# Row factors of blocks 2 and 3: from diagonal matrices on TensorE to a store in DRAM and a broadcast load

## The chip, the cores and the metric

The kernel runs on one core of one Trainium2 chip. The metric is device time in microseconds (us) of one execution; lower is better. Before the change three runs took 2093.21, 2093.47 and 2093.49 us, so the median is 2093.47 us. The engines are called PE (TensorE, matrix products), DVE (VectorE), ACT (ScalarE), POOL (GpSimd) and SP (SyncE, which here only issues DMAs).

## The reference

One layer of a pre-norm residual trunk over x of 2048 rows and 1024 columns, all in float32:

```python
h = rmsnorm(x, norm_mix_g)                      # x * rsqrt(mean(x*x) + EPS) * g, per row
u = einsum('bsd,dc->bsc', h, w_in)              # 1024 -> 3584 columns
gate_b, gate_c, v, x_r, g = split(u)
y_conv = gate_b * causal_dwconv(gate_c * v, conv_w)
y_rnn  = rg_lru(causal_dwconv(x_r, rnn_conv_w) + rnn_conv_b, ...) * gelu(g)
x = x + concat[rmsnorm(y_conv), rmsnorm(y_rnn)] @ w_out
x = x + square(relu(rmsnorm(x) @ W1)) @ W2      # 1024 -> 4096 -> 1024
out = rmsnorm(x, final_norm_g)
```

What the change touches is the factor of the first `rmsnorm`: for each row s of x one number, rsqrt(mean of x[s]^2 + EPS).

## The kernel before, in words

The 2048 rows are cut into four blocks of 512 (`TB`), and the blocks are worked in two pairs, (0, 1) and then (2, 3). Each pair goes through the mixers, the product with `w_out`, and the MLP (`mlp(b, ...)` with b = 0 and b = 2). The MLP of the first pair is the time from about 466 to 1066 us; it has an "up" half (`Up`, product with W1, matmuls on line 653) and a "down" half (`Down`, product with W2, line 771). Each matrix product is made of seven smaller products over the two blocks of a pair instead of eight (the numbers `i` in `ORDER = (1, 2, 6, 5, 7, 3, 4)`), and each of these of three passes over a high and a low part of the float32 operands (`w_hi`, `w_lo`, `z_hi`, `z_lo`, `H`), which ACT casts and DVE subtracts (`split_into`, lines 197 and 198). The loop of the up half is `for n in range(...)` over 56 pairs (s, i); its last seven, n = 49 to 55, belong to s = 7, and one of them is 24 matmuls.

While the MLP of the first pair runs, work for the second pair is put in between. One part of it is the row factors of blocks 2 and 3. The table `FACTORS` says at which n of the up half what is done: `next_rows(k, part)` loads a quarter of the rows of block k (tile `xq`), `next_part(k, 0..3)` lets ACT square and sum it, and `next_part(k, 4)` makes the factors (`norm_rows`, seven tiny DVE instructions and a root on ACT, ending in tile `rs_x`, 128 partitions x 4: row t*128 + p of the block is at partition p, column t).

The second pair's normalization works on the transposed rows `xT`, with the 512 rows of a block along the free dimension and the same factor wanted on all 128 partitions. So the factors have to be turned from 128 x 4 into one row of 512 and repeated on every partition (`bcs`, one tile of 128 x 512 for each of the two blocks). Before the change `next_part(k, 6)` makes four diagonal matrices (`diagonal`, lines 410 and 411 on DVE, high and low part, tiles `diag_hi` and `diag_lo` out of the pool `temp`), and `next_part(k, 8)` multiplies a matrix of ones with them on PE (`spread`, line 428, two matmuls into a PSUM tile `bc`) and lets ACT copy the result into `bcs` (line 1018). The consumer, `next_scale` (line 1021, instructions on line 435), runs near the end of the first pair's MLP.

What sets the order: inside `mlp` PE's order is the order of the code (`manual_schedule` for PE alone); the order of DVE, ACT, POOL and SP is chosen by the framework's scheduler when the kernel is built. Every engine then takes its instructions strictly in that order. SP issues nearly all DMAs through one queue: the spills `d_z<-snap` and `d_z<-z` of the up half (line 581), the weight loads `w<-in_w_mlp_in_dram` (line 613), and a background stream of loads and stores that prepares the second pair's weights (`prepare_sums`, lines 1624 and 1636, tiles `w_in`, `sum_hi`, `d_sum`). An instruction of SP that waits holds up all DMAs behind it. Tiles of `temp` come out of a pool of 27, weight tiles (`wtile`) out of 15, PSUM tiles out of 4.

Of the kernel before, what the change touches and what calls it, by code (L numbers as in the profile page):

```python
# [9 lines left out]
F32 = mybir.dt.float32  # L10
# [5 lines left out]
P = 128  # L16
# [3 lines left out]
TB = 512  # L20
NB = SEQ // TB
NT = TB // P
# [36 lines left out]
FACTORS = {}  # L59
for k in range(2):  # L60
    for n in range(4):
        FACTORS.setdefault(12 + 8 * n + 4 * k, []).append((True, 2 + k, n))
        FACTORS.setdefault(17 + 8 * n + 4 * k, []).append((False, 2 + k, n))
    for n in range(3):
        FACTORS.setdefault(46 + k + 2 * n, []).append((False, 2 + k, 4 + 2 * n))
PAIR_UNITS = "c0 g1 v0 x0 x1 x2 g0 x3 g2 b0 g3 c1 v1 b1".split()
PAIR_ITEMS = "c0.0 g1.0 bc1 hv00 hv0.0 G1.0 g1.1 G0.0 c0.1 x0.1 x1.1 v0.1 G0.1 x2.1 G1.1 x2.0 "
PAIR_ITEMS += "g0.1 x3.1 G2.0 x3.0 g2.1 g2.0 G2.1 b0.1 G3.0 b0.0 g3.1 G3.1 c1.0 g3.0 v1.0 b1.0 "
# [23 lines left out]
def block_kernel(  # L92
# [14 lines left out]
    nc = tc.nc  # L107
# [16 lines left out]
    dp = ctx.enter_context(  # L124
        tc.tile_pool(name="dp", bufs=2, space=bass.MemoryType.DRAM)
    )
# [14 lines left out]
    def psum(name, shape=(P, 2, TB)):  # L141
        return psp.tile(list(shape), F32, tag="ps", name=name)
# [4 lines left out]
    def small(name):  # L147
        return sp.tile([P, NT], F32, tag=name, name=name)
# [274 lines left out]
    def spread(diag, n, ps=None):  # L423

        if ps is None:
            ps = psum("bc", (P, n * P))
        for i, d in enumerate(diag):
            nc.tensor.matmul(
                ps, ones_r, d.rearrange("p n q -> p (n q)"), start=i == 0, stop=i == 1
            )  # L430
        return ps
# [13 lines left out]
    with tc.manual_schedule(  # L445
# [10 lines left out]
        for q in range(4):  # L456
            n, ks = q // 2, slice(2 * (q % 2), 2 * (q % 2) + 2)
# [38 lines left out]
        diag = diagonal(norm_rows(s2, NT), NT)  # L496
# [491 lines left out]
    bcs = [cp.tile([P, TB], F32, name="bcs%d" % i) for i in range(2)]  # L988
    factors = {}
    nxt = {}  # L990
# [9 lines left out]
    def next_part(b, n, ps=None):  # L1000

        nxt = factors.setdefault(b, {})
        if n == 0:
            nxt["s2"] = [small("s2_%d%d" % (b == NB - 1, i)) for i in range(2)]
        if n < 4:
            th, dh = n // 2, n % 2
            r = nxt.pop(n)
            for k in range(2):
                c = 2 * th + k
                nc.scalar.activation(  # L1010
                    r[:, k], r[:, k], AF.Square, accum_out=nxt["s2"][dh][:, c : c + 1]
                )
        elif n == 4:
            nxt["rs"] = norm_rows(nxt["s2"], NT)
        elif n == 6:
            nxt["diag"] = diagonal(nxt["rs"], NT)
        elif n == 8:
            nc.scalar.copy(bcs[b == NB - 1], spread(nxt["diag"], NT, ps))

    def next_scale(b, q):  # L1020
        scale_rows(xtt[b, q], 2 * q, bcs[b == NB - 1], 2)
# [1415 lines left out]
    def mlp(b, ups, r0, r1, t2, rest, xs, turns_at, prepared):  # L2437
        Z = {}
        in_mlp.append(b)
        seq = [(s, i) for s in range(3) for i in ORDER[:2]]  # L2440
        seq += [(s, i) for s in range(3) for i in ORDER[2:]]
        seq += [(s, i) for s in range(3, NS) for i in ORDER]
        downs = [Down(s) for s in range(NS // 2)]
        for n in range(-LEAD1, len(seq)):
            m = n + LEAD1
            if prepared <= m < len(seq):
                ups[seq[m][0]].prepare(seq[m][1])
            m = n + SUMS1
            if 0 <= m < len(seq):
                ups[seq[m][0]].sums(seq[m][1])  # L2450
            if n == -LEAD1:
                if prepared < 3:
                    ups[1].load((0,))
                ups[0].load((1,))
            if n < 0:
                continue
            s, i = seq[n]
            ups[s].multiply(i, H)
            if s == NS - 1 and i in (3, 4):
                with tc.issue_after(made_at["snap"]):  # L2460
                    downs[0].prepare(1, i - 3)
            ups[s].drain(i, Z)
            if n == 0:
                ups[2].load((0,))
            for t in turns_at.get(n, ()):
                rest(t, xs[t])
            if n == 4:
                ups[1].load((1,))
            later_operands(n, r0, r1, t2)
            if i == 5 and s >= 2 and s + 1 < NS:  # L2470
                ups[s + 1].load()
            if b < PAIRED:
                for fn, k, at in FACTORS.get(n, ()):
                    (next_rows if fn else next_part)(k, at)
            if b < PAIRED and BG_FROM <= n < len(seq) - 6 and i != 3:
                step()
            if i == 3 and s == 0:
                ups[2].load((1,))
            if s == NS - 1:
                if i in (1, 2):  # L2480
                    if i == 2:
                        downs[0].fetch(1, 0, Z)
                        downs[0].fetch(1, 1, Z)
                    downs[0].load(i - 1, hp.tile([P, 4, 2, 512], F32, tag="h", name="w2_first"))
                if i == 6:
                    downs[0].fetch(2, 0, Z)
                    downs[0].fetch(2, 1, Z)
                if i == 5:
                    downs[0].sums(0)
                if i == 7:  # L2490
                    downs[0].sums(1)
                    downs[0].fetch(6, 0, Z)
                if i == 3:
                    for th in range(2):
                        xt[b, th, 0] = refill("x2", keep_x[b, th, 0])

        more = b + 2 < NB
        seq = [(s, i, a) for s in range(NS // 2) for i in ORDER for a in range(2)]
        fetched = 5
        for n in range(-LEAD2, len(seq)):  # L2500
            m = n + LEAD2
            if m < len(seq):
                s, i, a = seq[m]
                if m > 1:
                    downs[s].prepare(i, a)
                if s and a == 0 and i in (1, 2):
                    downs[s].sums(i - 1)
                if a == 0 and i in (6, 5):
                    downs[s].last_sum(i == 5)
            for at, bb, dh in ((1, b, 1), (3, b + 1, 1), (9, b + 1, 0)):  # L2510
                if n == at:
                    for th in range(2):
                        xt[bb, th, dh] = refill("x2", keep_x[bb, th, dh])
            if n < 0:
                continue
            while fetched < min(n + LEAD2 + 3, len(seq)):
                s, i, a = seq[fetched]
                downs[s].fetch(i, a, Z)
                fetched += 1
            s, i, a = seq[n]  # L2520
            end = s == NS // 2 - 1
            if not (end and i == 4):
                downs[s].multiply(i, a)
                if a == 1:
                    downs[s].drain(i, b)
            elif a == 1:
                downs[s].multiply_last((ends[1].tiles if more else ends[1].last_tiles)(ends[0]))
            if i == 7 and s + 1 < NS // 2:
                downs[s + 1].load(a)
            if more and n > 6 and (s < 2 or s == 2 and i != 4):  # L2530
                step()
            if more and s == NS // 2 - 1:
                if (i, a) == (6, 1):
                    load_xt(b + 2)
                    hw = first_operands()
                if i in (7, 3):
                    q = 2 * (i == 3) + a
                    next_scale(b + 2, q)
                    split_first(hw, q, xtt[b + 2, q])
                if (i, a) == (3, 0):  # L2540
                    load_xt(b + 3)
                if i == 4:
                    for q in (2 * a, 2 * a + 1):
                        next_scale(b + 3, q)
            if end and (i, a) == (5, 0):
                ends = [Finish(b, 0), Finish(b + 1, 1)]
                ends[0].first()
            if end and (i, a) == (3, 1):
                if more:
                    for t in range(NT):  # L2550
                        ends[0].add(t, None)
                else:
                    stated[0] = True
                    ends[0].halves()
            if end and (i, a) == (7, 1):
                ends[1].first()
        if more:
            xr0, xr1 = ([xtt[b + 2 + n, q] for q in range(4)] for n in range(2))
            xt2 = [temp("T2") for _ in range(2)]
            for q in range(2):  # L2560
                other_sums(xr0, xr1, xt2, q)
            split_pair(6, xt2)
            hs["r"] = xr0, xr1, xt2
# [61 lines left out]
```

## Time and profile before

| | |
|---|---|
| runs | 2093.21, 2093.47, 2093.49 us |
| profiled execution | 2093.85 us; 2092.0 us of it from the first to the last instruction (span) |
| PE busy | 2082.5 us of the span |
| DVE, ACT busy | 1621.5 us, 1143.4 us |
| DMA | 226 GB/s mean over the span |
| granted TensorE clock | 0.999 |

Lines of the profile read so: in a timeline, start and duration in us, engine, line of the kernel, operation, out<-in, and in brackets the idle time before it and what ended it; in a list of waits, total us, times, longest; SPq is the DMA queue of SP, and the duration there is that of issuing. `L653` is line 653 of the kernel.

### The profile page before, as it was taken

The numbers are of one execution on the slowest core, as the hardware profiler recorded it, in microseconds if no ns is written. First come the engines' busy times: TensorE is split into PE (matmuls) and PEld (weight loads), VectorE is DVE, ScalarE is ACT, GpSimd is POOL, SyncE is SP. The second block draws the span as 40 slices with busy tenths as digits, with TensorE's granted clock in tenths as the row PEclk, the third lists the DMA queues.
The fourth block names the chain that finished last, engine by engine and source line by source line (L and its number), as shares of the span: only waits on it lengthen the run. The fifth ranks groups of instructions, "written<-read, shape, count | busy, mean of one in ns | idle before, by whom it ended". The sixth has DMA issues, their size and how long they took to land.

```text
span 2092.0 us, 25032 instructions
## 1 busy us (share of the span) xinstructions
PE 2082.5 (100%) x9328; PEld 1714.5 (82%) x9328; DVE 1621.5 (78%) x1844; ACT 1143.4 (55%) x1509; POOL 47.3 (2%) x75
## 2 busy tenths in 40 slices
PE   9999999999999999999999999999999999999998
PEld 8888788888888888888888887888888888888887
DVE  5789898569776878999987776875875665887776
ACT  6789863377655544443555887235853333333344
POOL 0011000000000000000000100000000000000000
PEclk9999999999999999999999999999999999999999
DMA  9489688743788788777384557675343445844432
GB/s 341 163 295 331 240 329 344 267 164 116 262 313 285 263 296 306 266 288 280 121 312 164 209 181 270 243 271 181 131 181 119 166 158 211 328 165 151 141 121 81
DMA packets 198760, 473.56 MB, mean 226 GB/s; under 512 B 14960, under 2 KB 79472, under 8 KB 198640
## 3 DMA queue, kind: packets, MB, share of 16 engines
q1 hardware_dynamic: 197040, 467.25, 61.6%
q10 hardware_dynamic: 1568, 4.72, 0.6%
q8 instruction: 73, 1.20, 0.2%
q14 instruction: 47, 0.39, 0.1%
q0 software_dynamic: 32, 0.00, 0.0%
HBM read 313.58 MB, written 158.33 MB: 226 GB/s over the span
## 4 chain that ended last, share of the span: by engine, by line
PE 82%; DVE 7%; ACT 4%; issue 2%; DMA 1%; POOL 0%; SPq 0%; DVEq 0%; ACTq 0%; POOLq 0%
PE up L653 41%; PE dn L771 27%; PE wo_x L2082 6%; PE wo_w L2082 3%; PE wo_y L2082 2%; DVE xr L1289 1%; DVE v L1346 1%; PE ps_b L256 1%; ACT r L1310 1%; PE psri L1757 1%; DVE w_lo L1230 1%; ACT gi L1317 1%; PE ps_c L256 1%; PE ps_v L256 1%; PE dn L790 1%
## 5 line engine op out<-in xcount | busy, mean ns | idle before, releaser
L653 PE MATMUL up<-H,w_hi 128*128 128x512 f32 x2576 | 795.2, 390 | 0.1
L653 PEld LDWEIGHTS up<-H,w_hi 128*128 128x128 f32 x2576 | 482.3, 188 | 103.0 <-issue 1.8
L653 PE MATMUL up<-H,w_lo 128*128 128x512 f32 x1288 | 501.5, 389 | 0.0
L771 PE MATMUL dn<-w_lo,z_hi 128*128 128x512 f32 x864 | 336.2, 389 | 0.8 <-DVE w_lo L198 0.8
L771 PE MATMUL dn<-w_hi,z_lo 128*128 128x512 f32 x864 | 336.1, 389 | 0.0
L771 PE MATMUL dn<-w_hi,z_hi 128*128 128x512 f32 x864 | 336.1, 389 | 0.0
L653 PEld LDWEIGHTS up<-H,w_lo 128*128 128x128 f32 x1288 | 241.8, 188 | 51.3 <-DVE w_lo L198 1.0
L197 ACT CAST z_hi<-z 128x1024 fp32r<-128x1024 f32 x112 | 118.1, 1054 | 299.9 <-PE dn L771 243.1
L198 DVE TENSOR_TENSOR w_lo<-w,w_hi 128x1024 fp32r<-128x1024 f32 x156 | 190.0, 1220 | 73.5 <-ACT w_hi L197 25.2
L197 ACT CAST w_hi<-w 128x1024 fp32r<-128x1024 f32 x156 | 163.0, 1049 | 114.8 <-PE up L653 48.2
L771 PEld LDWEIGHTS dn<-w_lo,z_hi 128*128 128x128 f32 x864 | 162.2, 188 | 34.7 <-DVE w_lo L198 1.2
L771 PEld LDWEIGHTS dn<-w_hi,z_lo 128*128 128x128 f32 x864 | 162.2, 188 | 33.8
L771 PEld LDWEIGHTS dn<-w_hi,z_hi 128*128 128x128 f32 x864 | 162.2, 188 | 33.7
L803 DVE TENSOR_TENSOR x<-dn,x 128x1024 f32<-128x1024 f32 x108 | 130.9, 1218 | 19.1 <-PE dn L771 19.0
L198 DVE TENSOR_TENSOR z_lo<-z,z_hi 128x1024 fp32r<-128x1024 f32 x112 | 136.2, 1216 | 4.8 <-ACT z_hi L197 4.8
L2082 PE MATMUL wo_x<-w_o,y_hi 128*128 128x512 f32 x384 | 119.5, 392 | 0.0
L665 ACT COPY snap<-up 128x1024 f32<-128x1024 f32 x48 | 48.7, 1015 | 63.4 <-PE up L653 57.1
L2082 PEld LDWEIGHTS wo_x<-w_o,y_hi 128*128 128x128 f32 x384 | 71.0, 188 | 14.5 <-DVE x L2095 0.4
L2082 PE MATMUL wo_x<-w_o,y_lo 128*128 128x512 f32 x192 | 75.0, 390 | 0.0
L670 ACT ACTIVATE snap<-snap 128x1024 f32<-128x1024 f32 x33 | 35.0, 1060 | 60.0 <-DVE snap L694 22.1
L2082 PE MATMUL wo_w<-w_o,y_hi 128*128 128x512 f32 x192 | 59.1, 389 | 0.0
L198 DVE TENSOR_TENSOR w_lo<-t,w_hi 128x1024 fp32r<-128x1024 f32 x32 | 39.0, 1220 | 19.0 <-PE dn L771 14.3
(426 smaller groups left out, 3211.3 us busy)
## 6 DMA issues: line engine op xcount, KB each, us to landing
z<-d_z SPq DMA_DIRECT2D x112, 512.0 KB, 5.8
w_o<-d_sum SPq DMA_DIRECT2D x84, 512.0 KB, 7.0
w<-in_w_mlp_in_dram SPq DMA_DIRECT2D x64, 512.0 KB, 6.5
d_z<-snap SPq DMA_DIRECT2D x64, 512.0 KB, 3.2
d_sum<-sum_hi SPq DMA_DIRECT2D x49, 512.0 KB, 5.2
d_z<-z SPq DMA_DIRECT2D x48, 512.0 KB, 3.3
w<-in_w_mlp_out_dram SPq DMA_DIRECT2D x48, 512.0 KB, 8.4
raw<-in_w_in_dram SPq DMA_DIRECT2D x32, 512.0 KB, 7.0
```

The costliest lines, as they stand in the source:

```text
L197: nc.scalar.copy(hi, src)
L198: return (lo_engine or V).tensor_tensor(lo, src, hi.bitcast(F32), SUB).ins
L256: nc.tensor.matmul(ps[:, j, :], ws[k // 4][:, k % 4, j * P : (j + 1) * P], hs(k), start=k == 0 and i == 0, stop=k == KD - 1 and i == len(p ...
L653: nc.tensor.matmul(ps[:, j, :], ws[:, k, j * P : (j + 1) * P], hs(k), start=i in (1, 2, 5) and k == 0 and n == 0, stop=k == 3 and n == len ...
L665: made_at["snap"] = nc.scalar.copy(t, ps).ins
L670: nc.scalar.activation(t, t, AF.Relu)
L771: nc.tensor.matmul(ps[t // 2][:, t % 2, :], zs[:, p, t * P : (t + 1) * P], ws[:, p, :], start=i in (1, 2, 5) and a == 0 and p == 0 and n == 0,
L790: nc.tensor.matmul(self.x[t // 2][:, t % 2, :], zs[:, p, t * P : (t + 1) * P], ws[:, p, :], start=False, stop=a == 1 and p == 1 and n == 2 ...
L803: V.tensor_add(xt[b, th, dh], ps[th], xt[b, th, dh])
L1230: tt(lo, r, hi.bitcast(F32), SUB)
L1289: stt(o, x_in[:, j, k : k + TB], par("rnn_conv_w", 8 * k + c), o, MUL, ADD)
L2082: nc.tensor.matmul(ps[t // 2][:, t % 2, :], ys[:, j, t * P : (t + 1) * P], ws[:, j, :], start=first and n == 1, stop=final and n == 6 * le ...
```

## The change

The steps 6 and 8 of `next_part` go for blocks 2 and 3: no diagonal matrices, no matmuls, no copy out of PSUM. Instead, right after step 4, `send_row` stores the 128 x 4 factors into a row of 512 numbers in DRAM (`d_row`), transposing by the access pattern, and loads that row back with all 128 partitions reading the same 2 KB. Both DMAs go through SP's queue; the second needs the first to have landed. (Block 1's factors, which go through the same functions with n = 4 and 6 elsewhere, stay as they were.)

```diff
@@ FACTORS
-    for n in range(3):
-        FACTORS.setdefault(46 + k + 2 * n, []).append((False, 2 + k, 4 + 2 * n))
+    FACTORS.setdefault(46 + k, []).append((False, 2 + k, 4))
@@ next_part
         elif n == 6:
             nxt["diag"] = diagonal(nxt["rs"], NT)
-        elif n == 8:
-            nc.scalar.copy(bcs[b == NB - 1], spread(nxt["diag"], NT, ps))
+
+    def send_row(b):
+        d = dp.tile([TB], F32, name="d_row")
+        nc.sync.dma_start(d.rearrange("(t p) -> p t", p=P), factors[b]["rs"])
+        nc.sync.dma_start(bcs[b == NB - 1], d[None, :].broadcast_to([P, TB]))
@@ mlp
                 for fn, k, at in FACTORS.get(n, ()):
                     (next_rows if fn else next_part)(k, at)
+                    if at == 4 and not fn:
+                        send_row(k)
```

How the instructions move, in three places. On PE, in the up half of the first pair's MLP, the pair of `bc` matmuls of block 2 stood between product i = 2 and product i = 6 of s = 7 (that of block 3 stands 24 matmuls later). Before:

```order
L653 MATMUL up<-H_3706,w_hi 128x512 x2
L653 MATMUL up<-H_3706,w_lo 128x512
L428 MATMUL bc<-diag_hi,ones_r 128x512
L428 MATMUL bc<-diag_lo,ones_r 128x512
L653 MATMUL up<-H_3953,w_hi 128x512
L653 MATMUL up<-H_3955,w_hi 128x512
L653 MATMUL up<-H_3953,w_lo 128x512
```

After it the two products follow on each other; nothing else on PE is moved:

```order
L652 MATMUL up<-H_3706,w_hi 128x512 x2
L652 MATMUL up<-H_3706,w_lo 128x512
L652 MATMUL up<-H_3953,w_hi 128x512
L652 MATMUL up<-H_3955,w_hi 128x512
L652 MATMUL up<-H_3953,w_lo 128x512
```

On SP's queue, after the change, the store and the load of block 2 stand together, between the stores of a background sum and the spills of s = 6 (`rs_x` are the factors, `d_row` the row in DRAM, `bcs` the broadcast tile, `d_z` the spills):

```order
L580 DMA d_z<-snap 128x1024
L1638 DMA d_sum<-sum_hi 128x1024
L1638 DMA d_sum<-w_in 128x1024
L1019 DMA d_row<-rs_x 128x4x1
L1020 DMA bcs_403<-d_row 128x512
L580 DMA d_z<-z_5643 128x1024
L580 DMA d_z<-snap 128x1024
L994 DMA xq<-in_x_dram 128x2x512
```

Before, `d_z<-z` followed directly on `d_sum<-w_in`. For block 3, again on SP's queue after the change, the store and the load are apart, with a spill and two stores of the background stream between them:

```order
L612 DMA w_5841<-in_w_mlp_in_dram 128x4x256
L1626 DMA w_in<-in_w_in_dram 128x4x256
L1019 DMA d_row<-rs_x 128x4x1
L580 DMA d_z<-snap 128x1024
L1638 DMA d_sum<-sum_hi 128x1024
L1638 DMA d_sum<-s_5801 128x1024
L1020 DMA bcs_404<-d_row 128x512
L580 DMA d_z<-z_5941 128x1024
```

The rest of SP's queue keeps its order. On DVE sixteen small instructions go, and one drain of `up` (line 682) comes to stand behind two `w_lo` instead of ahead of them; on ACT the two copies go and a cast of `sum_hi` and one of `w_hi` change places.

## Prediction

> **What bounds the kernel now.** I read the page first, then the list of waits of PE, then the chain and the timelines of the stretch that the change touches.
>
> ```profile
> span 2092.0 us, 25032 instructions
> PE 2082.5 (100%) x9328; PEld 1714.5 (82%) x9328; DVE 1621.5 (78%) x1844; ACT 1143.4 (55%) x1509; POOL 47.3 (2%) x75
> PE 82%; DVE 7%; ACT 4%; issue 2%; DMA 1%; POOL 0%; SPq 0%; DVEq 0%; ACTq 0%; POOLq 0%
> ...
> PE start_x L450 <- POOL ones_raw L272: 1.1, 1, 1.1
> PE dn L771 <- DVE w_lo L198: 0.8, 1, 0.8
> ...
> 1807.29 0.50 PE L771 MATMUL dn<-w_lo,z_hi 128*128 128x512 f32 x1 [0.80 <-DVE w_lo L198]
> ```
>
> PE is busy for all but 9.5 us of the span, and the only wait inside it is one of 0.8 us, far behind the place of the change: the last row shows it, at 1807 us. So the changed stretch is worth what PE does in it. The chain of waits, cut to 640 to 740 us, says the same: it runs on PE alone, and the `bc` matmuls that go are links of it.
>
> ```profile
> 639.87 93.25 PE up L653 x411
> 733.12 0.48 PE bc L428 x2
> 733.60 5.49 PE up L653 x24
> 739.10 0.48 PE bc L428 x2
> ...
> 732.73 0.40 PE L653 MATMUL up<-H,w_lo 128*128 128x512 f32 x1
> 732.96 0.40 PE L428 MATMUL bc<-diag_hi,ones_r 128*128 128x512 f32 x1
> 733.20 0.40 PE L428 MATMUL bc<-diag_lo,ones_r 128*128 128x512 f32 x1
> 733.44 0.63 PE L653 MATMUL up<-H,w_hi 128*128 128x512 f32 x2
> ...
> 761.22 0.39 PE L771 MATMUL dn<-w_hi,z_hi 128*128 128x512 f32 x1
> ```
>
> The duration of a matmul (0.40 us) overlaps the next one; what counts is the distance of the starts, 0.24 us here, 93.25 / 411 = 0.227 us for the matmuls of `up`. The last row is the first matmul of the down half.
>
> **Part 1, PE: four matmuls go.** Two pairs of 0.48 us are 0.96 us, all of it on the path. The 24 matmuls between the pairs take 5.49 us instead of 24 x 0.227 = 5.45, so at most another 0.05 to 0.1 us may go with them. I take -0.96; bounds -1.05 and 0 (if a later wait takes it back). The two PSUM tiles that go free nothing, since PE waits for no drain in this stretch.
>
> **Part 2, DVE and ACT: off the path.** Rows of the tiles `diag_hi`, `diag_lo` and `bcs`, and the one wait that hung on them:
>
> ```profile
> L410 DVE TENSOR_SCALAR diag_hi<-ident,rs_x x16: 278/279/289, 28.4 to 732.1; 128x128 fp32r<-128x128 f32 x16
> L411 DVE SCALAR_TENSOR_TENSOR diag_lo<-ident,rs_x,diag_hi x16: 343/349/352, 28.8 to 734.3; 128x128 fp32r<-128x128 f32 x16
> L1018 ACT COPY bcs<-bc x2: 578/582/587, 734.4 to 739.6; 128x512 f32<-128x512 f32 x2
> ...
> ACT sum_hi L197 <- PE bc L428: 3.5, 1, 3.5
> ```
>
> Eight of each on DVE are 8 x (0.279 + 0.349) = 5.0 us, two copies on ACT 1.2 us, and ACT's cast of `sum_hi`, which waited 3.5 us for the matmul to give a slot of the pool back, starts earlier. None of it is on the path: PE had no wait on either engine here. So I put it at 0. Its cover is PE's own full queue; were that gone, 5.0 us of DVE would be the most it could be worth. The drain of `up` (line 682) that DVE now takes behind two `w_lo` costs nothing by the same count: the sixteen instructions ahead of it are gone, 5.0 us against 2.3 us for the two.
>
> **Part 3, SP: four DMAs come in.** The question is what they hold up. The factors are there in time, and the issue times of SP's queue show its gaps (timelines of DVE and of SP, and busy times by stretch, where the two last columns are the share of the DMA engines and GB/s):
>
> ```profile
> 665.62 0.16 DVE L386 TENSOR_TENSOR rs_x<-rs_s,rs_q 128x4 f32<-128x4 f32 x1
> 699.02 0.16 DVE L386 TENSOR_TENSOR rs_x<-rs_s,rs_q 128x4 f32<-128x4 f32 x1
> ...
> 677.05 0.43 SPq L1636 DMA_DIRECT2D d_sum<-sum_hi  x1
> 677.59 0.65 SPq L1636 DMA_DIRECT2D d_sum<-w_in  x1
> 686.80 0.32 SPq L581 DMA_DIRECT2D d_z<-z  x1
> ...
> 708.09 0.37 SPq L1624 DMA_DIRECT2D w_in<-in_w_in_dram  x1
> 714.94 0.34 SPq L581 DMA_DIRECT2D d_z<-snap  x1
> 715.33 0.43 SPq L1636 DMA_DIRECT2D d_sum<-sum_hi  x1
> 715.85 0.66 SPq L1636 DMA_DIRECT2D d_sum<-s  x1
> 723.01 0.32 SPq L581 DMA_DIRECT2D d_z<-z  x1
> ...
> 682.00:684.00 2.00, 2.00 (x11) 1.65 (x10) 2.00 (x3) 1.70 (x2) 0.00 (x0) 1.00 0.00 0
> 684.00:686.00 2.00, 2.00 (x10) 1.69 (x9) 2.00 (x3) 0.70 (x2) 0.00 (x0) 1.00 0.00 0
> ```
>
> Block 2: the factors exist at 665.8, the store comes up at 677.59 + 0.65 = 678.2, and the next DMA of the old order, `d_z<-z`, went out at 686.80, when DVE had made its data. So SP stood idle for 8.6 us, and the DMA engines were empty from 682 to 686. Into this gap must go: issuing the store, its landing, issuing the load. Block 3: the store comes up at 708.5 with its factors ready since 699.2; its load stands behind `d_sum<-s`, at 716.5, so the store has 8.0 us to land with SP not waiting for it, and after that 6.5 us of gap remain before 723.01.
>
> No store of 4-byte pieces is in the trace, so its price is bounded by the nearest rows (the list of DMA issues with KB and us to landing; the DMA queue):
>
> ```profile
> prm<-in_rows_t_dram SPq DMA_DIRECT2D x1, 52.0 KB, 2.4
> gm<-in_mlp_g_t_dram POOLq DMA_DIRECT2D x1, 4.0 KB, 3.9
> w<-in_w_mlp_in_dram SPq DMA_DIRECT2D x64, 512.0 KB, 6.5
> gain<-in_final_norm_g_dram SPq DMA_DIRECT2D x4, 512.0 KB, 4.5
> q1 hardware_dynamic: 197040, 467.25, 61.6%
> ```
>
> Below: 2.4 us, a small transfer with 128 pieces. Above: 6.5 us, the `w` loads, which consist of 512 pieces (128 x 4 rows of 1 KB) like the store and move 256 times its bytes in a busy queue. A check by packets: 61.6% of 16 engines' 2092 us for 197040 packets is 0.105 us a packet; 512 packets over 16 engines are 32 x 0.105 = 3.3 us, and the bytes of the `d_sum` ahead need until 682. I take 6.5, the row with the same number of pieces. Then the load of block 2 goes out at 678.2 + 0.5 + 6.5 = 685.2 and is issued by 685.7, 1.1 us ahead of `d_z<-z`: cost 0. For block 3 the store has landed by 715.5, ahead of 716.5: cost 0. The loads are bounded by `gain`, a broadcast to 128 partitions like them with twice the bytes, 4.5 us; nothing waits for them, since `bcs` is first read at 999.7:
>
> ```profile
> L435 DVE SCALAR_TENSOR_TENSOR xT<-xT,prm,bcs x16: 737/742/747, 999.7 to 1057.5; 128x512 f32<-128x512 f32 x16
> ```
>
> A rule speaks against this. The Trainium skill, "DMA: Bandwidth & Descriptors", sections "Rules for kernel authors" and "Specifications": a last dimension that is not contiguous becomes one descriptor per element, and pieces under 512 B make the DMA engine read, modify and write. By its fixed cost of 2.0 us and its floor of 10.5 ns a packet the store would be an estimate of 2.0 + 512 x 0.0105 = 7.4 us, which would bring the load of block 2 out at 686.1 and leave the sum as it is; no row here shows a 4-byte piece.
>
> What if SP is late all the same? Behind the load of block 2 stand the spills, an `xq` load, and the weight loads for s = 7. The first of their operands is ready here (DVE, the second of the two):
>
> ```profile
> 712.64 2.35 DVE L198 TENSOR_TENSOR w_lo<-w,w_hi 128x1024 fp32r<-128x1024 f32 x2
> ```
>
> It is there at 715.0, and PE begins product i = 1 of s = 7 two products ahead of the `bc` pair, at 733.1 - 48 x 0.227 = 722.2. That is 7.2 us of slack behind SP's 8.6 us.
>
> **Sum.** -0.96 (PE) + 0 (DVE, ACT) + 0 (SP) = -0.96 us. The profiled execution took 2093.85 us with a span of 2092.0, 0.38 us above the median of the runs; its time becomes 2092.9, and the median 2093.47 - 0.96 = **2092.5 us**. A difference below 0.2%, 4.2 us, counts as no change here.
>
> **Rivals.**
>
> *Given back* (2093.5 us). The 0.96 us is eaten by a new wait of PE of the size of the one that the trace has, 0.8 us at 1807 us. For it: DVE and ACT take their instructions in another order from 730 us on, just ahead of the down half. Against it: both engines lose work there, and that wait follows a chain that itself starts from PE and would move along with it.
>
> *A little more* (2091.6). The wait at 1807 us goes too: 2092.5 - 0.8 = 2091.7, and 0.1 from the slower matmuls between the pairs. For it: four slots fewer are drawn from the pool of 27. Against: the wait is a thousand us later. Faster by over 4.2 us has no source: PE's waits inside the span amount to 1.9 us.
>
> *Slower: the store holds up SP* (2102). The store of 512 pieces of 4 bytes lands late, SP's queue stands, and the weights of s = 7 are late. SP is late when the landing takes over 8.6 - 0.5 - 0.5 = 7.6 us, PE when it takes over 7.6 + 7.2 = 14.8 us, and the run is 4.2 us slower from 14.8 + 4.2 + 1.0 = 20 us on. With 25 us: PE 10.2 us late at s = 7, less 0.96, 2102.7; a second delay at block 3 would lie beside the first, as the store there has 8.0 + 6.5 us. For it: the smallest pieces in the trace are the 32 bytes of `gm`, eight times as long. Against it: 25 us would be (25 - 2.4) / 32 = 0.7 us a piece on each engine, seven times the mean packet of this trace, which carries 2.4 KB. The rule of the Trainium skill quoted above is the one that would bring this about.
>
> **How the numbers follow.** The forecast 0.66; given back 0.17; a little more 0.06; slower by SP 0.09; something that I don't see and that is faster by over 0.2%, 0.02. So within 0.2%: 0.89, slower 0.09, faster 0.02. The range goes from 2093.5 - 0.96 - 0.1 - 0.8 - 0.3 (the scatter of the runs) = 2091.3 to 2093.5 + 0.8 + 0.1 = 2094.4, a wait as long as the one at 1807 us with the gain gone; that holds the first three cases, 0.89, and leaves the slower one out.
>
> **What would show it.** Right: no `bc` rows at 733 and 739 us, PE's products on both sides at a distance of 0.227 us, the up half shorter by about 1 us and the down half beginning at 760.3 instead of 761.2; the load of `bcs` issued before `d_z<-z` is ready, so that this spill still waits for DVE; DVE with 5.0 us less in 729 to 736. Wrong: the store landing after more than 7.6 us, a wait of SP on it that ends later than DVE's `z`, a wait of PE on `w_lo` near 722 us or at the start of the down half near 761 us.

## The result: 5.9 us slower, and the profile after

| | before | after |
|---|---|---|
| median of the runs compared (9 each) | 2093.29 us (2092.73 to 2093.93) | 2099.22 us (2096.77 to 2100.66) |
| ratio, 95% interval | | 1.0028 (1.0019 to 1.0037) |
| span of the profiled execution | 2092.0 us | 2097.0 us |
| start of the down half | 761.22 us | 764.09 us |

The forecast was 2092.5 us, range 2091.3 to 2094.4. The change is slower by 5.9 us, and the range missed it. The first lines of the profile after, and the list of PE's waits (us in total, times, longest):

```profile
span 2097.0 us, 25005 instructions
PE 2083.3 (99%) x9324; PEld 1713.0 (82%) x9324; DVE 1618.4 (77%) x1828; ACT 1142.2 (54%) x1507; POOL 46.9 (2%) x75
...
PE dn L770 <- DVE w_lo L197: 1.9, 2, 0.9
PE up L652 <- DVE w_lo L197: 1.5, 2, 1.1
PE up L652 <- DVE snap L689: 1.3, 1, 1.3
...
PE up L652 <- ACT snap L664: 0.4, 1, 0.4
```

The four matmuls are gone (9324 instead of 9328), but PE now waits in four places inside the MLP of the first pair, where it waited nowhere before. (Of the two waits in the row `PE dn L770`, one of 0.9 us lies at 1812 us and is the old one, 0.8 us at 1807.) Where this comes from is seen on SP's queue (timeline of SP) and in the time that the two stores took:

```profile
677.72 1.15 SPq L1019 DMA_DIRECT2D d_row<-rs_x  x1
691.04 0.32 SPq L1020 DMA_DIRECT2D bcs<-d_row  x1
691.47 0.37 SPq L580 DMA_DIRECT2D d_z<-z  x1
...
692.41 0.92 SPq L994 DMA_DIRECT2D xq<-in_x_dram  x1
...
713.15 1.02 SPq L1019 DMA_DIRECT2D d_row<-rs_x  x1
...
DMA to landing us min/median/max: 12.9/13.1/13.2
```

The store of block 2, 2 KB in 512 pieces of 4 bytes, needed 12.9 us, that of block 3 13.2. SP stood behind the load until 691.04 and sent the spill `d_z<-z` at 691.47 instead of 686.80, 4.7 us late. For most of that time the DMA engines moved nothing (busy times by stretch of after; the last two columns are the DMA engines' share and GB/s), from 682 to 690:

```profile
682.00:684.00 2.00, 2.00 (x11) 1.65 (x10) 2.00 (x3) 1.83 (x2) 0.00 (x0) 1.00 0.00 0
...
688.00:690.00 2.00, 2.00 (x10) 1.66 (x9) 2.00 (x3) 1.44 (x2) 0.00 (x0) 1.00 0.00 0
```

Part of that stretch, 682 to 686, was empty before too; then `d_z<-z` went out. The chain of waits of after, cut to the stretch from 640 to 800 us (start, duration, what), leads from that store to PE:

```profile
677.72 12.94 DMA d_row<-rs_x
...
691.47 4.64 DMA d_z<-z
...
696.24 1.24 DVE z L709
...
698.76 7.67 DMA d_sum<-w_in
706.45 4.96 DMA w_in<-in_w_in_dram
...
712.74 12.22 DMA w_in<-in_w_in_dram
...
725.05 0.06 DVE w_in L1658
...
727.41 1.15 DVE snap L693
728.58 1.07 ACT snap L669
...
736.53 27.72 PE up L652 x120
```

The late spill gives its slot back late, so DVE's next `z` starts late; the next spill, the stores of the background sum behind it, and the loads of `w_in` into their slots follow late; and the second `w_in` load takes 12.22 us where it took 6.8 before, beside the store of block 3. DVE and ACT take their work in order, so drains of PSUM (`snap<-up`, lines 689 and 693) and casts of weights stand behind instructions that wait for these transfers (waits of DVE and of ACT between 675 and 745 us):

```profile
DVE w_in L1658 <- DMA w_in<-in_w_in_dram: 4.3, 1, 4.3
DVE z L709 <- DMA d_z<-z: 3.2, 1, 3.2
...
ACT xq L1009 <- DMA xq<-in_x_dram: 6.8, 1, 6.8
```

None of these three waits is in the same list of the kernel with 16-byte pieces in natural order (below), whose load goes out at 682. The drain that PE waits for at 717 (line 690 before, 689 after) begins 4.7 us later than before (timelines of DVE, before and after):

```profile
711.51 1.21 DVE L690 TENSOR_TENSOR snap<-up,snap 128x1024 f32<-128x1024 f32 x1
...
716.16 1.22 DVE L689 TENSOR_TENSOR snap<-up,snap 128x1024 f32<-128x1024 f32 x1
```

What PE loses is read from the distance of the starts in its timeline, since a matmul should follow 0.227 us after the last one (0.45 after a row of two):

```profile
715.85 0.39 PE L652 MATMUL up<-H,w_lo 128*128 128x512 f32 x1
717.52 0.70 PE L652 MATMUL up<-H,w_hi 128*128 128x512 f32 x2 [1.28 <-DVE snap L689]
718.56 0.50 PE L652 MATMUL up<-H,w_lo 128*128 128x512 f32 x1 [0.34 <-DVE w_lo L197]
...
729.12 0.61 PE L652 MATMUL up<-H,w_hi 128*128 128x512 f32 x2
730.87 0.50 PE L652 MATMUL up<-H,w_lo 128*128 128x512 f32 x1 [1.13 <-DVE w_lo L197]
...
735.76 0.39 PE L652 MATMUL up<-H,w_lo 128*128 128x512 f32 x1
736.53 0.73 PE L652 MATMUL up<-H,w_hi 128*128 128x512 f32 x2 [0.38 <-ACT snap L664]
...
791.12 0.39 PE L770 MATMUL dn<-w_hi,z_lo 128*128 128x512 f32 x1
791.62 0.50 PE L770 MATMUL dn<-w_hi,z_hi 128*128 128x512 f32 x1
793.07 0.50 PE L770 MATMUL dn<-w_lo,z_hi 128*128 128x512 f32 x1 [0.95 <-DVE w_lo L197]
```

At 717: 1.67 - 0.23 and 1.04 - 0.45, together 2.0 us. At 731: 1.75 - 0.45 = 1.3. At 736: 0.77 - 0.23 = 0.5. At 792: 0.50 + 1.45 - 0.45 = 1.5. That is 5.3 us, with about 0.1 more behind each restart. The bracket shows less than PE loses each time, since the first matmuls after a wait also start further apart. With the restarts that is 5.7 us; less the 0.96 us of the four matmuls it leaves 4.7 of the 5.0 us by which the span grew.

### The profile page after: what moved, and what is told of

The parts are those of the page before. It is cut to its first block, busy times and chain, and to the rows that moved or that the text cites. A ratio compares the mean times of both kernels' runs of the same rounds, so it can differ in the third digit from the quotient of the medians.

```text
span 2097.0 us, 25005 instructions
## 1 busy us (share of the span) xinstructions
PE 2083.3 (99%) x9324; PEld 1713.0 (82%) x9324; DVE 1618.4 (77%) x1828; ACT 1142.2 (54%) x1507; POOL 46.9 (2%) x75
## 4 chain that ended last, share of the span: by engine, by line
PE 80%; DVE 7%; ACT 4%; DMA 3%; issue 2%; SPq 0%; POOL 0%; DVEq 0%; ACTq 0%; POOLq 0%
PE up L652 39%; PE dn L770 26%; PE wo_x L2084 6%; PE wo_w L2084 3%; PE wo_y L2084 2%; DVE xr L1291 1%; DVE v L1348 1%; DMA w_in<-in_w_in_dram 1%; PE ps_b L255 1%; ACT r L1312 1%; PE tps L1972 1%; DMA z<-d_z 1%; DMA d_row<-rs_x 1%; PE psri L1759 1%; DVE w_lo L1232 1%
## 5 line engine op out<-in xcount | busy, mean ns | idle before, releaser
L770 PE MATMUL dn<-w_lo,z_hi 128*128 128x512 f32 x864 | 336.4, 389 | 1.9 <-DVE w_lo L197 1.9
L770 PE MATMUL dn<-w_hi,z_hi 128*128 128x512 f32 x864 | 336.3, 389 | 0.3 <-ACT w_hi L196 0.2
L770 PE MATMUL dn<-w_hi,z_lo 128*128 128x512 f32 x864 | 336.1, 389 | 0.0
L770 PEld LDWEIGHTS dn<-w_lo,z_hi 128*128 128x128 f32 x864 | 162.2, 188 | 36.5 <-DVE w_lo L197 2.7
L770 PEld LDWEIGHTS dn<-w_hi,z_hi 128*128 128x128 f32 x864 | 162.2, 188 | 34.8 <-ACT w_hi L196 1.1
L770 PEld LDWEIGHTS dn<-w_hi,z_lo 128*128 128x128 f32 x864 | 162.2, 188 | 33.4
L669 ACT ACTIVATE snap<-snap 128x1024 f32<-128x1024 f32 x33 | 35.0, 1060 | 66.1 <-DVE snap L693 30.2
```

The source lines that it names most:

```text
L669: nc.scalar.activation(t, t, AF.Relu)
L770: nc.tensor.matmul(ps[t // 2][:, t % 2, :], zs[:, p, t * P : (t + 1) * P], ws[:, p, :], start=i in (1, 2, 5) and a == 0 and p == 0 and n == 0,
```

## The experiments

Each was timed in five rounds beside the kernel before, except the probe, which ran once. The medians of before lie at 2093.5 to 2093.6 us in all three groups, so 2092.5 means the gain that was forecast.

**The load later, away from the store.** The stores stay as they are; both loads are issued in the down half.

```diff
-        nc.sync.dma_start(bcs[b == NB - 1], d[None, :].broadcast_to([P, TB]))
+        sent[b] = d
...
+    def load_row(b):
+        with tc.issue_after(made_at["sp"]):
+            nc.sync.dma_start(bcs[b == NB - 1], sent[b][None, :].broadcast_to([P, TB]))
...
+            if more and n in (14, 16):
+                load_row(2 + (n == 16))
```

> The two broadcast loads move from SP's place behind the stores to the down half (some 100 us later, still long before 999 us, where bcs is read); the stores of 4-byte pieces stay where they are. Theory H (SP's queue stands, waiting for the store to land, and everything behind the load is late): the whole loss goes and the 0.96 us of the four matmuls remain, 2092 to 2093 us. Theory C (the small pieces clog the DMA engines, so that transfers behind the store land late, whoever waits): the part at block 3, where three stores landed 5.5 to 6.9 us late with nobody waiting for the row, stays, 2094 to 2098 us. Theory R (the loss comes from the new order on DVE and ACT and the other slots of the pool): about 2099 us.

Measured: 2092.59 us (2091.51 to 2095.27), ratio 0.9995 (0.9987 to 1.0004), span 2090.0. The stores still took 13.0 and 10.9 us. The spill goes out on time again, and PE's list of waits holds nothing but the start of the kernel (timeline of SP, waits of PE):

```profile
686.98 0.32 SPq L580 DMA_DIRECT2D d_z<-z  x1
...
PE start_x L449 <- POOL ones_raw L271: 1.1, 1, 1.1
PE start_x L481 <- ACT w_hi L464: 0.4, 1, 0.4
```

So here the stores of 13.0 and 10.9 us cost nothing that can be measured, since no instruction of SP waits for them.

**The removed part alone.** `send_row` does nothing, and `bcs` isn't filled with the factors of blocks 2 and 3.

```diff
+    nc.gpsimd.memset(bcs[1], 1.0)
...
-        d = dp.tile([TB], F32, name="d_row")
-        nc.sync.dma_start(d.rearrange("(t p) -> p t", p=P), factors[b]["rs"])
-        nc.sync.dma_start(bcs[b == NB - 1], d[None, :].broadcast_to([P, TB]))
+        pass
```

> The diagonals, the four matmuls and the two copies are gone as in the changed kernel, and the four DMAs are left out too; bcs holds constants (ones and the factors of block 1), so the factors of blocks 2 and 3 are left out of the computation. It measures the removed part by itself. Theories H and C: 2093.3 - 0.96 = 2092.3 us (bounds 2091.3 to 2093.3). Theory R: 2097 to 2100 us, since the order on PE, DVE and ACT is that of the changed kernel.

Measured: 2092.91 us (2091.57 to 2093.26), ratio 0.9995 (0.9987 to 1.0004), span 2089.8, down half from 759.56 us. DVE's and ACT's new order is that of the change, and no cost of it shows.

**The stores alone, beside the kernel before.**

```diff
                     (next_rows if fn else next_part)(k, at)
+                    if at == 4 and not fn:
+                        d = dp.tile([TB], F32, name="d_row")
+                        nc.sync.dma_start(d.rearrange("(t p) -> p t", p=P), factors[k]["rs"])
```

> The kernel before, with its diagonals and matmuls, and beside them only the two stores of 512 pieces of 4 bytes, at the places in SP's queue that they have in the changed kernel. Nothing reads the rows and nothing waits for them. Theory H: no loss, 2093.3 us (to 2094). Theory C: the transfers behind the stores land late as in the changed kernel, 2095 to 2099 us, and in the profile the stores d_z and d_sum behind the second one take 8 to 11 us instead of 2.6 to 4.2.

Measured: 2093.95 us (2093.13 to 2098.48), ratio 1.0004 (0.9995 to 1.0013). The stores took 13.1 and 12.3 us, and spills near them 5.6 and 6.9 us instead of 3.0 and 2.6, but PE waits for none of it. Contention by the store alone doesn't explain the 5.9 us.

**Pieces of 16 bytes, the row in another order.** Each partition writes its four factors side by side (128 pieces); DVE reads `bcs` with a step of four numbers to undo the order.

```diff
-        nc.sync.dma_start(d.rearrange("(t p) -> p t", p=P), factors[b]["rs"])
+        nc.sync.dma_start(d.rearrange("(p t) -> p t", t=NT), factors[b]["rs"])
...
+        f = bcs[b == NB - 1].rearrange("q (p t) -> q t p", t=NT)
...
```

> The changed kernel with the row in DRAM kept in the order (partition, column): the store then consists of 128 pieces of 16 bytes instead of 512 of 4, and the consumer on DVE reads bcs with a stride of four numbers. If the landing goes by the number of pieces, it falls from 13 us to 3 to 5 us, under the 7.6 us at which SP becomes late, and the time is 2092 to 2093 us. If it goes by their being small at all (under 512 bytes), it stays at 8 to 13 us and the time at 2096 to 2100 us. A slow read on DVE would show as more than 0.74 us on each of the sixteen instructions at 1000 to 1057 us and cost no more than 1 us.

Measured: 2094.75 us (2093.18 to 2095.47), ratio 1.0005 (0.9995 to 1.0014). The stores land in 3.7 and 6.5 us, and SP isn't held (`d_z<-z` at 687.02). But the consumer became slow, and PE waits behind it (group of line 1026, which is line 435 before; waits of PE):

```profile
L1026 DVE SCALAR_TENSOR_TENSOR xT<-xT,prm,bcs x16: 1116/1133/1172, 998.9 to 1059.4; 128x512 f32<-128x512 f32 x16
...
PE dn L789 <- DVE x L824: 1.9, 2, 1.4
```

1133 ns instead of 742 is 16 x 0.39 = 6.3 us more on DVE, between 1000 and 1060 us, where DVE is busy for 56.1 of 60 us already. PE lost about 2 us by it where I had expected 1 at most. The Trainium skill ("SBUF — State Buffer", in the part on the DMA port swizzle) says that SBUF serves full bandwidth only to consecutive accesses in one 16-byte line; a step of four numbers takes a new line each time, and the row agrees in direction; the page gives no price. The same note gives 4 float32 as how far one can step for free, which the row, at a step of exactly 4, doesn't bear out.

**Pieces of 16 bytes, natural order.** Instead, the rows of x are loaded so that partition p holds rows 4p to 4p + 3; the consumer stays as it was.

```diff
...
-            r, x[r0 : r0 + 256, c0 : c0 + 512].rearrange("(t p) d -> p t d", p=P)
...
+        v = x[r0 : r0 + TB, c0 : c0 + 512].rearrange("(p t) d -> p t d", t=NT)
...
+        nc.sync.dma_start(r, v[:, t0 : t0 + 2, :])
...
-        nc.sync.dma_start(d.rearrange("(t p) -> p t", p=P), factors[b]["rs"])
+        nc.sync.dma_start(d.rearrange("(p t) -> p t", t=NT), factors[b]["rs"])
```

> The quarters of the rows of blocks 2 and 3 are loaded so that partition p holds rows 4p to 4p+3 (xq's access pattern), and the store writes 128 pieces of 16 bytes in the row's natural order; the load and the consumer stay as in the change. Theory 'SP's queue stands behind the load that waits for the store': the store lands in about 3.7 us (block 2) and 6.5 us (block 3), as in the run with 16-byte pieces, so the load of block 2 goes out near 683, d_z<-z near 687 as before the change, PE has no wait in the MLP of the first pair, and the time is 2092.5 (2092.0 to 2093.3). Rival 'a DMA of this kind in SP's queue costs by itself': 2097 to 2100 as with the change. xq's pieces stay 2 KB, so its loads should take what they took.

Measured: 2092.09 us (2091.17 to 2093.24), ratio 0.9993 (0.9984 to 1.0002), span 2090.6. Stores 3.7 and 6.5 us; the consumer 750 ns; no wait of PE in this MLP (timelines of SP and DVE):

```profile
682.00 0.32 SPq L1021 DMA_DIRECT2D bcs<-d_row  x1
686.43 0.32 SPq L580 DMA_DIRECT2D d_z<-z  x1
...
711.57 1.22 DVE L689 TENSOR_TENSOR snap<-up,snap 128x1024 f32<-128x1024 f32 x1
```

This kernel does what the change set out to do. Its median lies 1.4 us below that of before; the interval does not quite exclude no change. The last row gives a slack that I had not looked for: the drain is done at 712.8, and PE wants the PSUM tile at 715.85 + 0.23 = 716.1 (the row of after), 3.3 us later.

**One load late, the other as in the change.** First block 3's load alone in the down half, then block 2's alone (`if b != 3:` or `if b != 2:` ahead of the load in `send_row`).

> The change, with block 3's load alone moved to the down half (n = 14); block 2's store and load stay together in SP's queue. If block 2's hold (d_z<-z 4.7 us late) is what costs: most of the loss stays, 2096 to 2099. If each block's hold costs its share: about 2096, and 2096 with the other block alone too. If block 3's hold is what costs: 2092.5 to 2093.5.

> The change, with block 2's load alone moved to the down half; block 3's store and load stay as in the change, with three DMAs between them. If block 2's hold is what costs: 2092.5 to 2094, since at block 3 the store has 8 us of its own and SP 6.5 us of idle time behind that. If block 3's hold costs its share: 2095 to 2097. If block 3's alone: 2097 to 2099.

Measured: with block 2's load left in place 2098.53 us (2096.37 to 2099.65), ratio 1.0024 (1.0014 to 1.0034); with block 3's left in place 2091.91 us (2091.23 to 2093.94), ratio 0.9995 (0.9986 to 1.0004). Without block 2's hold there is no loss.

**The loads on POOL's queue.**

```diff
-        nc.sync.dma_start(bcs[b == NB - 1], d[None, :].broadcast_to([P, TB]))
+        nc.gpsimd.dma_start(bcs[b == NB - 1], d[None, :].broadcast_to([P, TB]))
```

> The change, with both loads of bcs issued by POOL, whose queue holds nothing else until about 1080 us; the stores of 512 pieces of 4 bytes stay on SP. Theory 'SP stands behind the load': the stores land in 13 us as with the change, POOL stands for them instead of SP, d_z<-z goes out near 687, and the time is 2092.5 (2092.0 to 2094). Rival 'the DMA engines' standing during the store costs': 2097 to 2100, since the transfers meet the same store at the same time.

Measured: 2094.63 us (2092.83 to 2096.26), ratio 1.0006 (0.9997 to 1.0015). The stores took 12.8 us, POOL stood for them, `d_z<-z` went out at 686.87, and PE waits only 0.6 us in this MLP. Most of the loss is gone with the same stores in the same place. The median is 0.6 us above the range that I gave and some 2 us above the other kernels that hold nothing. The profiled executions differ by as much (span 2092.1, against 2090.0 with both loads late). Of that, 0.6 us is the wait in this MLP, 0.9 the wait near 1807 us that the kernel before has too, and 0.7 a longer wait at the start of the kernel. The `w_in` load beside block 3's store took 11.2 us; whether the 0.6 us comes from it wasn't tried.

**Stores alone on the chip.** The same 2 KB in several shapes, one store after the other, each made twice.

```diff
+        nc.sync.dma_start(d.rearrange("(t p) -> p t", p=P), s4)    # d_dense
+        nc.sync.dma_start(d.rearrange("(p t) -> p t", t=4), s4)    # d_sixteen
...
+            d = dp.tile([512, gap], F32, name="d_gap%d%s" % (4 * gap, rep))
...
+            nc.sync.dma_start(v[:, :, 0], s4)
```

> Stores alone, one after the other with the rest of the chip idle; nothing of the reference is computed and the output is zeros. Each of six stores is made twice: 512 pieces of 4 bytes, dense and transposed, as in the change (d_dense); 128 pieces of 16 bytes (d_sixteen); 256 pieces of 4 bytes with 128 of 8 bytes (d_half); 128 pieces of 4 bytes with 128 of 12 bytes (d_quarter); 512 pieces of 4 bytes spaced 64 bytes (d_gap64) and 512 bytes (d_gap512), each behind a store of the whole tile. If the landing goes by the number of pieces: dense, gap64 and gap512 alike at 8 to 13 us, half (256 pieces) about 5 to 8, sixteen and quarter (128 pieces) 2 to 4. If several small pieces in one memory line are what costs (each rewrites the line): gap512 clearly shorter than dense, 3 to 6 us against 8 to 13. If it is the busy queue of the kernel that made it 13 us: dense lands in 3 to 6 us here.

The list of DMA issues (KB each, us to landing):

```profile
d_densea<-s SPq DMA_DIRECT2D x1, 2.0 KB, 10.9
d_sixteena<-s SPq DMA_DIRECT2D x1, 2.0 KB, 1.4
d_gap64a<-s SPq DMA_DIRECT2D x1, 2.0 KB, 1.9
...
d_denseb<-s SPq DMA_DIRECT2D x1, 2.0 KB, 9.3
...
d_gap512b<-s SPq DMA_DIRECT2D x1, 2.0 KB, 1.8
```

512 pieces of 4 bytes land in 1.9 us when they are 64 bytes apart in DRAM, and in 9.3 to 10.9 when they lie side by side. So neither the number of pieces nor their size alone makes the store slow: their distance in DRAM matters too. Lying side by side isn't the whole of it either, since 128 pieces of 16 bytes side by side, also from different partitions, take 1.4 us. My other expectations fall: it isn't the busy queue, and not the count. The pair of 256 pieces of 4 and 128 of 8 bytes took 7.7 and 8.1 us, that of 128 pieces of 4 and 128 of 12 bytes 7.4 to 8.6, hardly less. Nor is it the time that the pieces themselves take: the first dense store is issued at 2.36 us, all its 528 packets are on record before 4 us, none from 4 to 13, and it lands at 13.3. So some 9 us pass behind the last packet; in the change, too, no packet is on record from 682 to 690 us. The Trainium skill ("DMA: Bandwidth & Descriptors", section "Specifications") says that pieces under 512 B make the engine read, modify and write; pieces of one size differ here by a factor of 5, so the size alone doesn't decide. One thing differs besides the distance: the spaced rows had been written as a whole just before. What happens in these 9 us isn't shown by these rows.

**Only block 3 with 16-byte pieces.** Block 2 as in the change.

```diff
...
+        if b != 3:
+            v = x[r0 : r0 + TB, c0 : c0 + 512].rearrange("(t p) d -> p t d", p=P)
...
+        if b == 3:
+            nc.sync.dma_start(d.rearrange("(p t) -> p t", t=NT), factors[b]["rs"])
+        else:
+            nc.sync.dma_start(d.rearrange("(t p) -> p t", p=P), factors[b]["rs"])
```

> Block 2 as in the change (512 pieces of 4 bytes, load behind it); block 3's rows are loaded so that its store writes 128 pieces of 16 bytes. SP should issue block 2's load near 691, and d_z<-z some 4.5 us later than without the change. Theory 'two losses': in the change PE loses first where a drain of up on DVE (line 689) comes late behind the late background sum, some 2 us near 717, and again near 731 to 737 and 792, because block 3's store of 4-byte pieces makes the w_in load beside it take 12.2 us: then only the first is left, 2094 to 2096. Theory 'block 2's hold is all': 2097.5 to 2099.5, as with block 3's load late.

Measured: 2094.22 us (2091.92 to 2095.86), ratio 1.0003 (0.9994 to 1.0012). The DMA issues of the two kernels at block 3, first two rows of after, then two of this one, and then PE's timeline of this one:

```profile
w_in<-in_w_in_dram SPq DMA_DIRECT2D x1, 512.0 KB, 12.2
d_row<-rs_x SPq DMA_DIRECT2D x1, 2.0 KB, 13.2
```

```profile
w_in<-in_w_in_dram SPq DMA_DIRECT2D x1, 512.0 KB, 6.8
d_row<-rs_x SPq DMA_DIRECT2D x1, 2.0 KB, 6.6
...
719.01 0.70 PE L652 MATMUL up<-H,w_hi 128*128 128x512 f32 x2 [1.76 <-DVE snap L689]
720.05 0.50 PE L652 MATMUL up<-H,w_lo 128*128 128x512 f32 x1 [0.34 <-DVE w_lo L197]
...
791.84 0.50 PE L770 MATMUL dn<-w_lo,z_hi 128*128 128x512 f32 x1 [0.95 <-DVE w_lo L197]
```

The waits at 731 and 736 are gone, those at 717 and 792 remain. So the loss has two parts (medians; the kernel before had 2093.48, 2093.52 and 2093.29 us beside the three): block 2's hold costs 2094.22 - 2092.09 = 2.1 us against the kernel with 16 bytes at both blocks, and the store of block 3 with its 4-byte pieces puts 2099.22 - 2094.22 = 5.0 us on top, but only when the queue is late already, since with block 2's load moved away it cost nothing. These sizes are rough: the runs of a kernel with such waits scatter by 4 us, and by the spans of the profiled executions (2090.6, 2094.1 and 2097.0) the parts are 3.5 and 2.9. Nor does the store stretch the `w_in` load by itself. Issued 0.4 us ahead of the same store of 4-byte pieces, this load took 6.8 us with both loads late and with the stores beside the kernel before, 8.4 with block 2's load late, and 12.6 with block 3's late. What decides isn't shown. One part of my expectation was wrong: I had put the wait at 792 down to block 3's store too.

**Half and double the store of block 2.** With block 3 in 16-byte pieces, block 2's store is made as 256 pieces of 4 bytes and 128 of 8, or made twice into two rows.

```diff
+            nc.sync.dma_start(d.rearrange("(t p) -> p t", p=P)[:, 0:2], rs[:, 0:2])
+            nc.sync.dma_start(d[256:TB].rearrange("(p t) -> p t", t=2), rs[:, 2:4])
...
+            e = dp.tile([TB], F32, name="d_more")
+            nc.sync.dma_start(e.rearrange("(t p) -> p t", p=P), factors[b]["rs"])
```

> As the kernel with block 3 in 16-byte pieces, and block 2's store made as two: 256 pieces of 4 bytes and 128 pieces of 8 bytes (the rows of its second half are loaded to match). Alone on the chip such a pair landed in 8 us where 512 pieces took 9.3 to 10.9; here I expect 10 to 11 us instead of 13, so that d_z<-z is 2 to 3 us late instead of 4.5. If the slack of PE behind it is the 3.3 us that the drain of line 689 has (ready at 712.8, wanted at 716.1): 2092.5 to 2093.3. If every us that SP stands counts: 2094 to 2096.

> As the kernel with block 3 in 16-byte pieces, and block 2's factors are stored twice, each in 512 pieces of 4 bytes, into two rows; the load reads the second. It should go out near 700 (22 us after the store), d_z<-z about 13 us late. By the prediction's slack (SP 7.6 us, PE 7.2 us more): 22 - 14.8 = 7 us of loss, 2099 to 2100. By the drain's slack of 3.3 us behind SP's: 13 - 3.3 = 10 us and the restarts, 2102 to 2105. If block 2's hold does not cost PE its own length: below 2099.

Measured: half 2092.72 us (2091.90 to 2093.32), ratio 0.9996 (0.9987 to 1.0005). The later of its stores took 9.0 us, the load went out at 688.51 and `d_z<-z` at 688.93, 2.1 us late; DVE came to the drain of line 689 at 713.93, and PE has no wait in this MLP: 2.1 us of lateness are inside the slack of 3.3, and the rival "every us that SP stands counts" falls. Double 2095.97 us (2094.40 to 2097.03), ratio 1.0012 (1.0003 to 1.0021): the test didn't do what it was meant for, as the two stores landed side by side in 13.2 and 12.7 us and the load went out at 692.25, not at 700. Its profile has the wait for the drain (1.2 us) but none at 792, so that one doesn't follow from the hold alone. How the loss grows with longer holds stays open.

## Why the prediction was wrong, point by point

- **Part 1 (PE, -0.96 us): right, as far as the runs can tell.** The kernels without a hold and with the old consumer (load late, removed part alone, 16 bytes in natural order, block 2's load late) lie at 2091.9 to 2092.9 us, 0.7 to 1.6 below the before of their group, with the down half from 759.6 to 760.4 us instead of 761.2. No single one is told from no change; the four together point one way. The loads on POOL's queue, 2094.63 us, don't. The spans, 2089.8 to 2090.8 us instead of 2092.0, say a little less than they seem to: in the two shortest the wait of 0.8 us at 1807 is gone or down to 0.2, without a change there.
- **Part 2 (DVE, ACT, 0): right** by the kernel with the removed part alone.
- **Part 3, the landing: this step failed first.** I bounded it by 2.4 and 6.5 us and took 6.5, from loads with as many pieces; it measured 12.9 and 13.2. The number of pieces was the wrong thing to match: 512 pieces of 4 bytes land in 1.9 us when they are spaced. The packet check (3.3 us) priced the packets, which are through within 2 us on the idle chip, and left out the 9 us behind them. The estimate by the Trainium skill's page, 7.4 us, was nearer and still short; the page gives its two figures for DMAs issued from GpSimd, and this store goes out from SP. The 7.6 us from which SP is late were about right: 12.9 - 7.6 = 5.3 us, and the spill was 4.7 us late.
- **The slack behind SP: this step failed too.** I took 7.2 us from one `w_lo`, so PE should have been late only from a landing of 14.8 us on. What came late first was a PSUM drain on DVE (line 689) behind the background's `w_in`, which the prediction's list of what stands behind the load doesn't have; its slack is 3.3 us. With the load out 10.2 us after the store's start (half the store) PE lost nothing, with 12.8 us (block 3 alone in 16-byte pieces) it did.
- **Block 3 ("cost 0", "a second delay would lie beside the first"): wrong.** The 8.0 + 6.5 us of gap held for the store's own landing (with block 2's load moved away this block is free). But beside the store of 4-byte pieces the `w_in` load took 12.2 us instead of 6.8, and behind a queue that was late already PE felt it.
- **The rivals.** The slower one had the mechanism right and the point wrong: 4.2 us slower only from a landing of 20 us on. Its chance of 0.09 rested on that point. "Given back" and "a little more" didn't occur: the wait at 1807 us stayed, and what came anew was far larger than the 0.96 us.

## What to carry to other kernels

Before a DMA that waits for another one is put into a shared in-order queue, look for its price in a row with the same layout at the destination, not the same number of pieces, and if there is none, widen the bound. The slack behind a queue is the smallest over everything that it feeds (slots given back by spills, background loads, PSUM drains behind them on an in-order engine), not that of the operand nearest to the change. And let a partition write 16 bytes in a row instead of four times 4, or issue the dependent load later or from an idle queue.

## What I had not expected of the hardware

- 512 pieces of 4 bytes side by side: 9.3 to 10.9 us on an idle chip, 10.9 to 13.2 in the kernel, with no packet of any DMA on record from 682 to 690 us in the kernel and from 4 to 13 us on the idle chip; the same pieces 64 bytes apart 1.9 us (rows just written as a whole), 128 pieces of 16 bytes 1.4 us (3.7 and 6.5 in the kernel).
- A transfer of 512 KB issued 0.4 us ahead of such a store landed in 11.2 to 12.6 us in three kernels, in 8.4 in one, and in two in the 6.8 us that it takes without the store.
- Two such stores at once took no longer than one: 13.2 and 12.7 us.
